# Hybrid mLSTM and S5 step: four edits, the last normalisation step of the heads moved to VectorE among them

## The chip, the cores and the metric

The program runs on one core of a Trainium2 chip. The metric is the device time of one execution in microseconds; the median of three runs of the kernel before stands for it. The engines are TensorE (PE), VectorE (DVE), ScalarE (ACT), GpSimd (POOL) and SyncE (SP). PEld is TensorE's loading of weights, which overlaps its matmuls. SP computes nothing: it issues all transfers (DMAs) of this program.

## What is computed

A decoder layer over 1024 prompt tokens and 8 × 4 sample tokens, in float32, with an mLSTM half (4 heads of 128) and an S5 half (32 groups of 16 channels):

```python
a = rmsnorm(h, ln_mix)                      # h * rsqrt(mean(h*h) + 1e-6) * ln_mix
x_m, z_m, o_m, i_pre, f_pre, x_s, z_s = split(a @ w_in)
x_conv, conv_new = causal_conv(x_m, state_conv, conv_w, conv_b)   # conv_new: the last 3 rows of x_m
x_conv = silu(x_conv)
hA, C1, n1, m1 = mlstm_chunkwise(q, k, v, i_t, logf, C0, n0, m0)  # h = num / max(|qn|, exp(-m))
hA = hA * sigmoid(o_m)
hA = (hA - mean(hA)) * rsqrt(var(hA) + EPS) * ln_head             # per head
hA = (hA + skip_a * x_conv) * silu(z_m)
yB, sre1, sim1 = s5_scan(x_s, ...)
yB = gelu(yB); yB = yB * sigmoid(yB @ w_glu + b_glu) * silu(z_s)
h = h + concat(hA, yB) @ w_out
h = h + sigmoid(h @ w_ple_gate) * rmsnorm(p @ w_ple, ln_ple)
```

The final rmsnorm of h and the new states are the outputs.

## The kernel before

Products with weights are made of three matmuls: a weight and its operand are each split into a rounded high part and the rest (`mm3`, L122 to L125: high·high, low·high, high·low). ACT writes the high part, POOL or DVE subtracts it from the raw tile for the low one (L115, L116, and `wload`, L1342 and L1345).

The stages follow one another:

- **Start.** Nine row tiles of x are loaded, normalised and transposed (`x_tile`, L150 to L180). The first tile comes in two halves (ACT squares L164, DVE and POOL make the factor `rr` L166 to L168, DVE multiplies by `rr` and by `ln_row` L170); later tiles go in one piece (ACT L157, then `rsqrt`, a DVE step L55 and a POOL power L56, then DVE L159). PE transposes into `tpx` (L176), ACT and DVE split into `aTh` and `aTl` (L178, L179), and the projection o (`ps_o`) begins. `ln_row` holds ln_mix on all 128 partitions: one DMA of 512 KB reads the same row 128 times (L297), between the loads of the first x tile and of the first weights `raw_o`.
- **S5, units u = 0 to 7.** Per unit DVE builds tables, PE transposes them (`s5_in`, tile `tpW`, L561), scans run on DVE, DVE writes the state tile `xs_` (L645, L646), PE multiplies it out into `py` (L655, L656). Between these PE has other work from a list of fillers (projection matmuls), in measured helpings: FILL_A, FILL_B and FILL_C columns (`take`). After some units a step of the generator `gate` runs (`if u in (0, 1, 4, 6): next(gate)`), which turns the gate values into tables. Its step after u = 4 copies the sample tokens' gates into `gs` (L798, L799), transposes them with PE into `tps` (L803), copies them out with DVE into `sr` (L804), and transposes three more tiles into `tpk` (L807). `tps` lies in the PSUM pool psT (one buffer) that `tpW` uses as well; `tpk` lies in psG (one buffer).
- **mLSTM heads,** the pair (0, 1) and then (2, 3) (`turns`), with the sample heads between them. After its chunks a head is normalised by `lnorm`: reciprocal of the denominator, DVE's statistics (L1209, L1211), small vectors (L1212 to L1216, with `rsqrt` on DVE and POOL inside), and last a pass over the 128x128 tiles, out = in · scale + bias with a scale and a bias per partition, on ACT (L1218), eight chunks per head in two halves of four. PE transposes the result (`tph`, L1180), DVE adds the skip part (`sk`, L1183). The conv state of the prompt, three columns per head, is copied by DVE out of `xm` into `pcn` (L1102); `xm` is itself loaded from the DRAM tile `d_xm`.
- **GLU.** Matmuls into `ps_g`, ACT's tanh `tg` (L1040), DVE (L1042), POOL's product `zg` (L1044), and at the end of a column block ACT's `mXh` (L1055) and DVE's `mXl` (L1056).
- **Output.** w_out, then w_ple and w_ple_gate over eight row tiles, with their weights loaded and split ahead.

The order of instructions on every engine is fixed when the program is built, by a scheduler that plays the program through with estimated times; on PE the S5 and mLSTM stages are in the order of the code instead. All DMAs go through the one queue of SP in that fixed order, so a transfer that waits for its data holds up those behind it.

Of the kernel before, what the change touches and what calls it, by code (L numbers as in the profile page):

```python
# [8 lines left out]
F32 = mybir.dt.float32  # L9
# [20 lines left out]
def tile_hymba(ctx: ExitStack, tc: tile.TileContext, d: dict, o: list):  # L30
# [4 lines left out]
    def dma(out, in_):  # L35
        nc.sync.dma_start(out, in_)  # L36
# [107 lines left out]
    def x_load(i):  # L144
        xt = xp.tile([128, 1024], F32, tag="xt", name="xt", bufs=5)
        for q in range(1 if i else 2):
            w = 1024 if i else 512
            dma(xt[:128 if i < 8 else 32, w * q:w * q + w], x_src(i)[:, w * q:w * q + w])
        return xt
# [143 lines left out]

    xts = []
    ow = []
    xts.append(x_load(0))
    dma(ln_row, bcast(d["ln_mix"], 1024))  # L297
    ow.append(o_w(0, 0))
    xts.append(x_load(1))
    ow.append(o_w(0, 1))  # L300
# [2 lines left out]
    dma(bgr[:, 0:4], bcast(d["b_igate"], 4))  # L303
    dma(bgr[:, 4:8], bcast(d["b_fgate"], 4))
    xts.append(x_load(3))
    for i in range(9):
        if i + 4 < 9:
            xts.append(x_load(i + 4))
        x_tile(i, xts[i])
        o_tile(0, ow, i)  # L310
        if i in (1, 4, 8):
            s5_x(0, LOC[i][0])
# [420 lines left out]
    def gates_g():  # L733
# [64 lines left out]
        V.tensor_copy(gs[:, 0], gates[:32, 0:4, 8])  # L798
        V.tensor_copy(gs[:, 1], lf[:32, :, 8])  # L799
        sr = gt_([4, 2, 32], "sr")  # L800
        tp = pt([4, 2, 32], "tps")
        for i in range(2):
            T.transpose(tp[:, i, :], gs[:, i, :], ident[:32, :32])  # L803
        V.tensor_copy(sr, tp)  # L804
        tp = pg([128, 3, 32], "tpk")
        for i, t_ in enumerate((g_, wl_, en_)):
            T.transpose(tp[:, i, :], t_, ident[:32, :32])  # L807
# [117 lines left out]
    with tc.manual_schedule(engines={mybir.EngineType.PE}):  # L925
        gate = gates_g()
        ins = [s5_in(u) for u in range(8)]
        outs = [s5_out(u) for u in range(8)]
        parts = {}
        runs = []  # L930

        def start(u, WV):
            runs.append(s5_run(u, WV, lambda: parts[u]))
            prod(runs[u])

        prod(ins[0])
        WV = prod(ins[0])
        prod(outs[0])  # L940
        tabs = prod(outs[0])
        with tc.high_priority():
            parts[0] = (*tabs, *s5_rot(0))
        start(0, WV)
        prod(ins[1])
        prod(outs[1])
        for u in range(8):
            prod(runs[u])
            if u < 7:
                WV = prod(ins[u + 1])  # L950
            take(FILL_A)
            if u < 7:
                start(u + 1, WV)
                tabs = prod(outs[u + 1])
                with tc.high_priority():
                    parts[u + 1] = (*tabs, *s5_rot(u + 1))
            if u < 6:
                prod(ins[u + 2])
            take(FILL_B)
            prod(runs[u])  # L960
            prod(runs[u])
            if u < 6:
                prod(outs[u + 2])
            take(FILL_C)
            if u in (0, 1, 4, 6):
                next(gate)
        end = s5_final()
        for n in (5000, 3000, 3000, 0):
            prod(end)
            if n:  # L970
                take(n)
# [102 lines left out]
    def mtile_xm(h):  # L1074
        xm = pxm.tile([128, 1027], F32, tag="xm", name="xm", bufs=2)
        V.memset(xm[:, 0:3], 0.0)
        dma(xm[:, 3:], d_xm[h])

        xc = (mlx if h < 2 else mly).tile([128, 1024], F32, tag="xc", name="xc", bufs=2)
        A.activation(xc, xm[:, 0:1024], AF.Identity, bias=cvb[:, h:h + 1], scale=cvw[:, h:h + 1])  # L1080
        for j in range(1, 4):
            V.scalar_tensor_tensor(xc, xm[:, j:j + 1024], cvw[:, 4 * j + h:4 * j + h + 1], xc, op0=MUL, op1=ADD)
        for q in range(2):
            tt_ = mlx.tile([128, 512], F32, tag="ctmp", name="ctmp", bufs=1)
            A.activation(tt_, xc[:, 512 * q:512 * q + 512], AF.Tanh)
            V.scalar_tensor_tensor(xc[:, 512 * q:512 * q + 512], tt_, 1.0, xc[:, 512 * q:512 * q + 512],
                                   op0=ADD, op1=MUL)
        yield
        v1 = ml.tile([128, 8, 129], F32, tag="v1", name="v1", bufs=2)
        V.memset(v1[:, :, 128:129], 1.0)  # L1090
        xmc[h] = (v1, xc)
        for t in range(2):
            ps = pv([128, 4, 128], "vps")
            for c in range(4):
                cc = 4 * t + c
                T.matmul(ps[:, c, :], xm[:, 3 + 128 * cc:131 + 128 * cc], wv[:, h, :], start=True, stop=True)
            A.copy(v1[:, 4 * t:4 * t + 4, 0:128], ps)
            yield

        V.tensor_copy(xsm[:, h, :, 0:3], scT[:, h, :].rearrange("p (b j) -> p b j", j=3))  # L1100
        V.tensor_copy(pcn[:, h, 0:24].rearrange("p (b j) -> p b j", j=3), xsm[:, h, :, 4:7])
        V.tensor_copy(pcn[:, h, 24:27], xm[:, 1024:1027])  # L1102
        a_ = ml.tile([128, 2, 8, 4], F32, tag="csm", name="csm", bufs=1)
        A.activation(a_[:, 0], xsm[:, h, :, 0:4], AF.Identity, bias=cvb[:, h:h + 1], scale=cvw[:, h:h + 1])
        for j in range(1, 4):
            V.scalar_tensor_tensor(a_[:, 0], xsm[:, h, :, j:j + 4], cvw[:, 4 * j + h:4 * j + h + 1], a_[:, 0],
                                   op0=MUL, op1=ADD)
        A.activation(a_[:, 1], a_[:, 0], AF.Tanh)
        V.scalar_tensor_tensor(xcs[:, h, :].rearrange("p (b t) -> p b t", t=4), a_[:, 1], 1.0, a_[:, 0],
                               op0=ADD, op1=MUL)  # L1110
        yield
# [88 lines left out]
    def lnorm(hs, qn, enm, p, n):  # L1200

        w_ = [ml.tile([128, n], F32, tag=f"ln{i}", name=f"ln{i}", bufs=2) for i in range(5)]
        V.scalar_tensor_tensor(w_[0], qn, -1.0, qn, op0=MUL, op1=MAX)
        V.tensor_tensor(w_[0], w_[0], enm, op=MAX)
        V.reciprocal(w_[0], w_[0])
        st_ = ml.tile([128, n, 6], F32, tag="bst", name="bst", bufs=2)
        mv = ml.tile([128, n, 2], F32, tag="bmv", name="bmv", bufs=2)
        for c in range(n):
            V.bn_stats(st_[:, c, :], hs[:, c, :])  # L1209
        for c in range(n):  # L1210
            V.bn_aggr(mv[:, c, :], st_[:, c, :])  # L1211
        V.scalar_tensor_tensor(w_[1], w_[0], 0.25, w_[0], op0=MUL, op1=MUL)  # L1212
        V.tensor_tensor(w_[1], w_[1], mv[:, :, 1], op=MUL)
        rsqrt(w_[2], w_[1], 1.0, EPS, w_[3])
        V.scalar_tensor_tensor(w_[2], w_[0], 0.5, w_[2], op0=MUL, op1=MUL)
        V.scalar_tensor_tensor(w_[4], mv[:, :, 0], -1.0, w_[2], op0=MUL, op1=MUL)  # L1216
        for c in range(n):
            A.activation(hs[:, c, :], hs[:, c, :], AF.Identity, bias=w_[4][:, c:c + 1], scale=w_[2][:, c:c + 1])  # L1218

    xmc = {}  # L1220

# [445 lines left out]
```

## Time and profile before

| | us |
|---|---|
| runs | 668.5, 662.63, 663.2 (median 663.2) |
| profiled execution, its own time | 665.62 |
| its span in the trace | 663.7 |
| PE busy | 611.8 (92%) |
| DVE busy | 441.0 (66%) |
| ACT busy | 266.1 (40%) |
| POOL busy | 147.6 (22%) |

The span begins with the first and ends with the last instruction of the trace; 1.9 us of the execution lie outside it. The mean granted clock of PE was 0.981. In the rows below a timeline row is one instruction, or several of a kind that follow each other (x4), with its start and its duration; in brackets stands how long its engine had been idle before it and what ended the wait. PEclk is the granted clock of PE as a share of full speed.

### The profile page before, as it was taken

The page shows a single profiled execution, that of the slowest core. Times are in us where ns is not written, and L with a number is a line of the kernel's source. Part 1 is how long each engine was busy: PE and PEld are TensorE (multiplying, and loading weights), DVE is VectorE, ACT ScalarE, POOL GpSimd, SP SyncE. Part 2 cuts the span into 40 slices and gives each one's busy share as a digit, 9 for nine tenths or more (in the row PEclk, how much of TensorE's full clock was granted, in tenths as well). Part 3 has the DMA queues.
Part 4 walks back from the last instruction along what each step waited for, and adds up shares of the span by engine and source line. Part 5 has one row for each costly group of instructions (what it writes and reads, how often), then busy time and mean ns, then how long its engine had stood idle before and what let it go on. Part 6 is the DMA issues. An engine that isn't in the chain of part 4 may idle for free. (4 is left out here: it accounts for less than half of the span.)

```text
span 663.7 us, 11597 instructions
## 1 busy us (share of the span) xinstructions
PE 611.8 (92%) x4068; PEld 538.3 (81%) x4068; DVE 441.0 (66%) x1297; ACT 266.1 (40%) x655; POOL 147.6 (22%) x165
## 2 busy tenths in 40 slices
PE   3999999999989998887989996899999999999995
PEld 2999998999979996776978796767888876788885
DVE  4877878999999944985657588834222335576444
ACT  5553743333434455444341536533112225443332
POOL 6730200000000003024323536842001113110000
PEclk9999999999989997998999997999999999999998
DMA  8811453455543439363634654766241273412111
GB/s 286 238 57 33 113 162 90 131 145 153 146 118 97 111 80 267 92 195 108 172 112 123 186 171 145 256 209 214 74 143 71 89 250 126 150 49 103 64 64 63
DMA packets 111983, 90.53 MB, mean 136 GB/s; under 512 B 33519, under 2 KB 94339, under 8 KB 111926
## 3 DMA queue, kind: packets, MB, share of 16 engines
q1 hardware_dynamic: 111926, 89.80, 45.2%
q8 instruction: 32, 0.52, 0.3%
q14 instruction: 25, 0.20, 0.1%
HBM read 62.19 MB, written 27.58 MB: 135 GB/s over the span
## 5 line engine op out<-in xcount | busy, mean ns | idle before, releaser
L1595 PE MATMUL po<-wgh,hTh 128*128 128x512 f32 (+1 forms) x136 | 52.3, 385 | 0.1
L1489 DVE TENSOR_TENSOR xt<-xt,po 128x512 f32<-128x512 f32 x16 | 11.0, 687 | 61.5 <-PE po L1488 58.1
L1596 PE MATMUL po<-wgl,hTh 128*128 128x512 f32 (+1 forms) x136 | 51.1, 378 | 0.0
L1597 PE MATMUL po<-wgh,hTl 128*128 128x512 f32 (+1 forms) x136 | 51.1, 379 | 0.0
L123 PE MATMUL ps_o<-hi_o,aTh 128*128 128x264 f32 (+2 forms) x136 | 41.0, 302 | 0.7 <-ACT aTh L178 0.7
L124 PE MATMUL ps_o<-lo_o,aTh 128*128 128x264 f32 (+2 forms) x136 | 39.8, 293 | 1.4 <-POOL lo_o L116 1.4
L125 PE MATMUL ps_o<-hi_o,aTl 128*128 128x264 f32 (+2 forms) x136 | 40.0, 294 | 0.2 <-DVE aTl L179 0.2
L123 PE MATMUL ps_zs<-aTh,hi_zs 128*128 128x256 f32 (+2 forms) x96 | 39.5, 411 | 0.0
L123 PE MATMUL ps_xm<-aTh,hi_xm 128*128 128x256 f32 (+2 forms) x96 | 34.8, 363 | 0.0
L123 PE MATMUL ps_zm<-aTh,hi_zm 128*128 128x256 f32 (+2 forms) x96 | 32.7, 341 | 0.0
L1488 PE MATMUL po<-woh,mlo 128*128 128x512 f32 x80 | 32.7, 409 | 0.0
L123 PE MATMUL ps_xs<-aTh,hi_xs 128*128 128x256 f32 (+2 forms) x96 | 31.4, 327 | 1.0 <-ACT xs L287 1.0
L1487 PE MATMUL po<-wol,mh 128*128 128x512 f32 x80 | 31.9, 398 | 0.0
L125 PE MATMUL ps_zm<-aTh,lo_zm 128*128 128x256 f32 (+2 forms) x96 | 31.7, 330 | 0.0
L124 PE MATMUL ps_zm<-aTl,hi_zm 128*128 128x256 f32 (+2 forms) x96 | 31.7, 330 | 0.0
L125 PE MATMUL ps_xm<-aTh,lo_xm 128*128 128x256 f32 (+2 forms) x96 | 31.5, 328 | 0.0
L1486 PE MATMUL po<-woh,mh 128*128 128x512 f32 x80 | 31.5, 394 | 0.0
L125 PE MATMUL ps_zs<-aTh,lo_zs 128*128 128x256 f32 (+2 forms) x96 | 31.4, 327 | 0.0
L124 PE MATMUL ps_zs<-aTl,hi_zs 128*128 128x256 f32 (+2 forms) x96 | 31.4, 327 | 0.0
L124 PE MATMUL ps_xm<-aTl,hi_xm 128*128 128x256 f32 (+2 forms) x96 | 31.4, 327 | 0.0
L124 PE MATMUL ps_xs<-aTl,hi_xs 128*128 128x256 f32 (+2 forms) x96 | 31.4, 327 | 0.0
L125 PE MATMUL ps_xs<-aTh,lo_xs 128*128 128x256 f32 (+2 forms) x96 | 31.1, 324 | 0.0
(591 smaller groups left out, 1923.5 us busy)
## 6 DMA issues: line engine op xcount, KB each, us to landing
xt<-in_x_prompt SPq DMA_DIRECT2D x15, 512.0 KB
Wraw<-in_w_out SPq DMA_DIRECT2D x16, 256.0 KB
Wraw<-in_w_ple_gate SPq DMA_DIRECT2D x16, 256.0 KB
d_h<-xt SPq DMA_DIRECT2D x8, 512.0 KB
h_t<-d_h SPq DMA_DIRECT2D x8, 512.0 KB
out<-g_t SPq DMA_DIRECT2D x14, 256.0 KB
mt<-d_m SPq DMA_DIRECT2D x10, 256.0 KB
d_us<-xs SPq DMA_DIRECT2D x32, 72.0 KB
```

What stands on the lines that cost most here:

```text
L123: T.matmul(ps, wh, xh, start=first, stop=False)
L124: T.matmul(ps, wh, xl, start=False, stop=False)
L125: last_mm[0] = T.matmul(ps, wl, xh, start=False, stop=last).ins
L1486: T.matmul(ps, mh[:, k % 4, :], hi, start=k == 4, stop=False)
L1487: T.matmul(ps, mh[:, k % 4, :], lo, start=False, stop=False)
L1488: T.matmul(ps, mlo[:, k % 4, :], hi, start=False, stop=k == 3)
L1489: V.tensor_tensor(xt[:, cs], xt[:, cs], ps, op=ADD)
L1595: T.matmul(ps[:, :b - a], hTh[i][:, k, :], hi[:, ws], start=k == 4, stop=False)
L1596: T.matmul(ps[:, :b - a], hTh[i][:, k, :], lo[:, ws], start=False, stop=False)
L1597: T.matmul(ps[:, :b - a], hTl[i][:, k, :], hi[:, ws], start=False, stop=k == 3)
```

## The change

There are four edits. (1) ln_mix is loaded once, 4 KB on one partition, and spread over 128 partitions by two matmuls with a column of ones; DVE copies the two halves from PSUM into `ln_row`. (2) The transposes of the sample gates are a step of `gate` of their own, one S5 unit earlier, and their PSUM tile comes from psG instead of psT. (3) The three conv state columns of each head come into `pcn` by a DMA from `d_xm` instead of a DVE copy out of `xm`. (4) The last step of `lnorm` is a `tensor_scalar` on DVE instead of an `activation` on ACT.

```diff
-    dma(ln_row, bcast(d["ln_mix"], 1024))
+    one_p = xp.tile([1, 128], F32, tag="xn", name="one_p", bufs=4)
+    V.memset(one_p, 1.0)
+    ln1 = xp.tile([1, 1024], F32, tag="xn", name="ln1", bufs=4)
+    dma(ln1, bcast(d["ln_mix"], 1024, 1))
...
     xts.append(x_load(3))
+    for q in range(2):
+        ps = pv([128, 512], "tpl")
+        T.matmul(ps, one_p, ln1[:, 512 * q:512 * q + 512], start=True, stop=True)
+        V.tensor_copy(ln_row[:, 512 * q:512 * q + 512], ps)
...
-        tp = pt([4, 2, 32], "tps")
+        tp = pg([4, 2, 32], "tps")
         for i in range(2):
             T.transpose(tp[:, i, :], gs[:, i, :], ident[:32, :32])
         V.tensor_copy(sr, tp)
+        yield
         tp = pg([128, 3, 32], "tpk")
...
-            if u in (0, 1, 4, 6):
+            if u in (0, 1, 3, 4, 6):
                 next(gate)
...
-        V.tensor_copy(pcn[:, h, 24:27], xm[:, 1024:1027])
+        dma(pcn[:, h, 24:27], d_xm[h, :, 1021:1024])
...
         for c in range(n):
-            A.activation(hs[:, c, :], hs[:, c, :], AF.Identity, bias=w_[4][:, c:c + 1], scale=w_[2][:, c:c + 1])
+            V.tensor_scalar(hs[:, c, :], hs[:, c, :], w_[2][:, c:c + 1], w_[4][:, c:c + 1], op0=MUL, op1=ADD)
```

Since the scheduler orders the engines anew, more moves than the edited lines. In the rows of the order, line numbers of the kernel after are 7 (up to L1102) or 8 higher than those of the kernel before.

On PE, after S5 unit 4, the kernel before has the sample transposes ahead of `tpk` and of the next unit's `tpW`:

```order
L125 MATMUL ps_zm_2622<-aTh_106,lo_zm_2518 128x416
L803 MATMUL tps<-ident,gs 4x32 x2
L807 MATMUL tpk<-ident,g__2031 128x32
L807 MATMUL tpk<-ident,wl__2056 128x32
L807 MATMUL tpk<-ident,en__2057 128x32
L561 MATMUL tpW<-ident,wt 128x128 x4
L123 MATMUL ps_zm_2780<-aTh_104,hi_zm_2776 128x256
L124 MATMUL ps_zm_2780<-aTl_107,hi_zm_2776 128x256
```

In the kernel after, the first piece is the end of unit 3 and the second the end of unit 4:

```order
L125 MATMUL ps_xm<-aTh_106,lo_xm_2320 128x416
L810 MATMUL tps<-ident,gs 4x32 x2
L568 MATMUL tpW<-ident,wt 128x128 x4
L123 MATMUL ps_zm_2538<-aTh_104,hi_zm_2534 128x256
L124 MATMUL ps_zm_2538<-aTl_107,hi_zm_2534 128x256
```

```order
L125 MATMUL ps_zm_2639<-aTh_106,lo_zm_2535 128x416
L815 MATMUL tpk<-ident,g__2040 128x32
L815 MATMUL tpk<-ident,wl__2065 128x32
L815 MATMUL tpk<-ident,en__2066 128x32
L568 MATMUL tpW<-ident,wt 128x128 x4
L123 MATMUL ps_zm_2789<-aTh_104,hi_zm_2785 128x256
```

The two transposes into `tps` have moved one unit up, ahead of an earlier `tpW`, and `tpk` has stayed.

On DVE, ahead of unit 5's second half of `xs_` (the row L646 before, L653 after), the kernel before has:

```order
L640 TENSOR_TENSOR v_2755<-zi,rti 128x256
L641 TENSOR_TENSOR v_2756<-zr,rti 128x256
L642 TENSOR_TENSOR v_2757<-zi,rtr 128x256
L822 TENSOR_TENSOR sg<-sr,sb 4x32
L551 TENSOR_TENSOR u_2928<-pdr,Cs 128x576
L552 TENSOR_TENSOR u_2929<-pdi,Cj 128x576
L645 TENSOR_TENSOR xs__2751<-v_2754,v_2755 64x2x128 x2
L716 SCALAR_TENSOR_TENSOR ztmp<-ztmp,zc 128x256
L599 TENSOR_TENSOR rti<-rBr,rAi 128x256
L599 TENSOR_TENSOR rtr<-rBr,rAr 128x256
L646 TENSOR_TENSOR xs__2751<-v_2756,v_2757 64x2x128 x2
```

and the kernel after:

```order
L647 TENSOR_TENSOR v_2764<-zi,rti 128x256
L648 TENSOR_TENSOR v_2765<-zr,rti 128x256
L649 TENSOR_TENSOR v_2766<-zi,rtr 128x256
L836 COPY smo<-sm__2722 4x8
L586 SCALAR_TENSOR_TENSOR ks<-dsel,Dt,ks 128x16
L558 TENSOR_TENSOR u_2937<-pdr,Cs 128x576
L559 TENSOR_TENSOR u_2938<-pdi,Cj 128x576
L1396 TENSOR_TENSOR smb<-smb,smask 32x128
L652 TENSOR_TENSOR xs__2760<-v_2763,v_2764 64x2x128 x2
L606 TENSOR_TENSOR rti<-rBr,rAi 128x256
L606 TENSOR_TENSOR rtr<-rBr,rAr 128x256
L653 TENSOR_TENSOR xs__2760<-v_2765,v_2766 64x2x128 x2
```

A copy of the sample gates' result (`smo`), `ks` and the sample mask (`smb`, which is loaded from DRAM) now stand ahead of unit 5's `xs_`; the sample gates' scan `sM` has gone further ahead, to the unit before.

On ACT, at the end of the second pair of heads, the kernel before has the two halves of L1218 among the tanh of the GLU and the weight casts `woh`:

```order
L1040 ACTIVATE tg<-ps_g,hcols 128x288
L1306 COPY sob<-tpn 32x128
L1218 ACTIVATE qd<-qd,ln_5205,ln_5203 128x128 x4
L1342 CAST woh_5756<-Wraw 128x512
L1218 ACTIVATE qd<-qd,ln_5244,ln_5242 128x128 x4
L1473 CAST mh<-mt 128x512
L1055 ACTIVATE mXh_5352<-zg 128x1024
L1040 ACTIVATE tg<-ps_g,hcols 128x288
```

and the kernel after:

```order
L1048 ACTIVATE tg<-ps_g,hcols 128x288
L1314 COPY sob<-tpn 32x128
L1350 CAST woh_5765<-Wraw 128x512
L1481 CAST mh<-mt 128x512
L1063 ACTIVATE mXh_5361<-zg 128x1024
L1048 ACTIVATE tg<-ps_g,hcols 128x288
```

The two groups of four are gone, and `mh`, `mXh` and the next tanh follow directly on the casts. `mXh` still reads POOL's `zg`.

## Rows read from the trace of the kernel before

**Rows 1.** The page: busy time, share of the span and instructions of each engine.
```profile
PE 611.8 (92%) x4068; PEld 538.3 (81%) x4068; DVE 441.0 (66%) x1297; ACT 266.1 (40%) x655; POOL 147.6 (22%) x165
```

**Rows 2.** Windows: stretch in us, length, busy time (instructions) by engine, PEclk, DMA share, GB/s.
```profile
100.00:235.00 135.00, 131.86 (x1074) 125.38 (x1073) 130.87 (x344) 51.09 (x142) 0.63 (x6) 0.99 0.48 123
400.00:450.00 50.00, 38.76 (x324) 32.41 (x324) 36.22 (x62) 25.44 (x52) 33.97 (x29) 0.93 0.61 194
450.00:650.00 200.00, 199.68 (x1012) 158.95 (x1010) 84.23 (x152) 62.06 (x149) 28.24 (x31) 1.00 0.34 115
```

**Rows 3.** Timeline of PE, first 20 us: start us, us, instruction [idle before <-releaser].
```profile
13.69 0.59 PE L124 MATMUL ps_o<-lo_o,aTh 128*128 128x264 f32 x1 [1.44 <-POOL lo_o L116]
...
17.87 1.94 PE L176 MATMUL tpx<-ident,xn 128*128 128x128 f32 x8 [1.17 <-DVE rr L55]
```

**Rows 4.** Timeline of ACT, POOL and DVE in the same stretch.
```profile
10.06 1.07 ACT L115 CAST hi_o<-raw_o 128x1056 fp32r<-128x1056 f32 x1 [4.42 <-DMA raw_o<-in_w_in]
...
11.21 2.43 POOL L116 TENSOR_TENSOR lo_o<-raw_o,hi_o 128x1056 fp32r<-128x1056 f32 x1 [4.74 <-ACT hi_o L115]
...
14.19 2.45 POOL L116 TENSOR_TENSOR lo_o<-raw_o,hi_o 128x1056 fp32r<-128x1056 f32 x1
...
8.22 1.42 DVE L170 SCALAR_TENSOR_TENSOR xn<-xt,rr,ln_row 128x512 f32<-128x512 f32 x2 [2.39 <-DMA ln_row<-in_ln_mix]
...
14.18 3.54 DVE L159 SCALAR_TENSOR_TENSOR xn<-xt,rr,ln_row 128x1024 f32<-128x1024 f32 x1 [0.84 <-POOL rr L56]
```

**Rows 5.** S5 units 4 and 5: timeline of PE and DVE, one window.
```profile
187.84 0.66 PE L561 MATMUL tpW<-ident,wt 128*128 128x128 f32 x4 [2.92 <-DVE sr L804]
...
201.40 0.39 PE L655 MATMUL py<-us,tz 128*128 128x136 f32 x2
...
197.60 0.87 DVE L646 TENSOR_TENSOR xs__2751<-v,v 64x256 f32<-64x256 f32 x2
...
188.00:192.00 4.00, 4.00 (x23) 4.00 (x23) 4.00 (x9) 0.59 (x1) 0.00 (x0) 0.57 0.06 23
```

**Rows 6.** First pair of heads: timeline of PE.
```profile
290.51 0.36 PE L1292 MATMUL sups<-svm,skw 96*128 96x258 f32 x1 [1.60 <-DVE sc L1294]
...
302.91 1.48 PE L1180 MATMUL tph<-ident,qd 128*128 128x128 f32 x4 [3.35 <-ACT qd L1218]
...
305.32 1.09 PE L1180 MATMUL tph<-ident,qd 128*128 128x128 f32 x4
```

**Rows 7.** The same stretch: timeline of DVE and ACT, one window.
```profile
284.29 0.17 DVE L1102 COPY pcn<-xm 128x3 f32<-128x3 f32 x1 [1.47 <-DMA xm<-d_xm]
...
302.36 3.19 ACT L1218 ACTIVATE qd<-qd,ln,ln 128x128 f32<-128x128 f32 x8 [2.67 <-DVE ln L1216]
...
305.00:308.00 3.00, 2.96 (x11) 2.13 (x11) 1.10 (x3) 0.55 (x2) 3.00 (x3) 0.53 0.05 18
```

**Rows 8.** Second pair of heads, end: timeline of PE, ACT, POOL and SP.
```profile
407.90 0.61 PE L123 MATMUL ps_g<-yh,hi_g 128*128 128x288 f32 x1 [5.93 <-ACT tg L1040]
...
404.35 1.65 ACT L1218 ACTIVATE qd<-qd,ln,ln 128x128 f32<-128x128 f32 x4 [1.11 <-DVE ln L1216]
...
406.41 1.05 ACT L1055 ACTIVATE mXh<-zg 128x1024 fp32r<-128x1024 f32 x1
407.37 0.48 ACT L1040 ACTIVATE tg<-ps_g,hcols 128x288 f32<-128x288 f32 x1
...
402.55 1.65 POOL L1044 TENSOR_TENSOR zg<-tg,zg 128x256 f32<-128x256 f32 x2
...
436.32 0.39 SPq L36 DMA_DIRECT2D d_m<-zg  x1
```

**Rows 9.** Groups of instructions: count | busy us, mean ns; the last one with min/median/max ns.
```profile
L1218 ACT ACTIVATE qd<-qd,ln,ln 128x128 f32<-128x128 f32 x32 | 13.0, 484 | 4.9 <-DVE ln L1216 4.8
...
L1172 DVE SCALAR_TENSOR_TENSOR qd<-so,nu 128x128 f32<-128x128 f32 x32 | 8.8, 275 | 0.0
...
L1129 PE MATMUL qps<-xc,Gm x16: 590/592/1222, 255.2 to 364.6; 128*128 128x512 f32 x16
```

## Prediction

> **What bounds the kernel now.** I read the page first. PE is busy 611.8 of 663.7 us, so all its idle time together is 51.9 us, and no edit touches a large share of PE's work [rows 1]. What the change can win are PE's stops and the stretches at half clock behind them. The windows by stage come next. In the S5 stage PE and DVE are both nearly full (131.86 and 130.87 of 135 us); between 400 and 450 PE works 38.76 of 50; from 450 to 650 it works 199.68 of 200, so what is won or lost by 450 reaches the end one to one [rows 2]. The timeline of PE then gives the stops by place, and that of the engine named as releaser what it did before: the start [rows 3, 4], one S5 unit [rows 5], the first pair of heads [rows 6, 7], the end of the second pair [rows 8]. In all four places a line of the diff stands in or near the chain.
>
> **Edit 1, ln_mix.** It removes a 512 KB broadcast, for which DVE waited until 8.22 [rows 4]. It adds a 4 KB load, a memset, two fp32 matmuls of 128x512 and two DVE copies. The nearest row for the matmuls is L1129, 128x512 in two records of 0.59 us at full and up to 1.22 at half clock [rows 9]: 2.4 us each if the clock is still low, 4.9 for both, begun when the first weights are not there yet. The copies have DVE's half of a 1.42 us pair as the nearest row, 0.7 each [rows 4]. PE's first product that needs the low weights waits for POOL's `lo_o` (11.21 to 13.64), this for ACT's cast at 10.06, and this for the load of `raw_o` [rows 3, 4]. `raw_o`, as large as `ln_row` and behind it in the queue, landed 1.84 us after it [rows 4]; without those 512 KB I let it land 1.9 earlier. Next late are the two spread matmuls and copies: x's second half can be multiplied at about 10.2, transposed at 10.9 and cast at 12, a little ahead of what `lo_o` then needs. So the start gains at most 1.9, and loses 1 if the spread is slower than that. I take 1.3. The DVE work has cover, as DVE is idle in this stretch while it waits.
>
> **Edit 2, the sample transposes.** In S5 unit 4 PE stands 2.92 us at `tpW`, because `tps` held the one buffer of psT until DVE's late copy `sr`; then it runs at 0.57 of its clock for 4 us, mostly the lower level of 1.2 GHz, which costs 1.7 more [rows 5]. Both go with the edit: 4.6 us on PE, the upper end. But DVE is full in this stage. It ended unit 5's `xs_` at 198.47 and PE came to read it at 201.40 [rows 5], a slack of 2.9. If PE comes 4.6 earlier, at 196.8, `xs_` is what is late, and the changed order puts `smo`, `ks` and `smb` ahead of it, some 0.15 to 0.2 us each by rows of that size, and `smb` may wait for its load. So `xs_` ends near 199.3 and PE waits 2.5: 2.1 are left. If the clock falls again behind that wait, as it fell behind 2.92, another 1.7 goes, and 0.4 is left. I take 1.2, with 0 and 4.6 as ends.
>
> **Edit 3, the conv columns.** Four DVE copies of 0.17 go, one of which held DVE 1.47 us for the load of `xm`, in front of the products `sc` that PE's `sups` waits for [rows 6, 7]. Four DMAs of 1.5 KB come onto SP's queue, each some 0.4 us of issue like its neighbour [rows 8]; they read DRAM that the load of `xm` before them reads too, so they add no wait of their own, and `pcn` is used only at the end. Its gain is counted with the next edit, since both meet in the first pair of heads.
>
> **Edit 4, L1218.** ACT loses 32 instructions with 13.0 us and one more of the sample; eight in a row took 3.19, so each holds ACT 0.39 [rows 9, 7]. DVE gets 33 `tensor_scalar` of 128x128, which this trace does not have in float32 from SBUF at that size. From above, the nearest row is L1172, same size with two tensor inputs, 0.275 us [rows 9]; beside a running POOL instruction it can be more: L159 took 3.54 beside `lo_o`, where two halves of the same work took 1.42 without it [rows 4]; 0.275 stretched by that 2.5 is 0.7. From below I let it be half of 0.275, as if the second input cost half the time. I take 0.2, between them, 6.6 us in all, and 0.7 beside POOL. Off the stops it is hidden by DVE's idle time.
>
> The Trainium skill speaks against this edit here: the GPSIMD Engine Reference, under Specifications, says that POOL's way to SBUF is shared with VectorE and that the two contend where a DVE instruction runs in a two-port mode or has two SBUF inputs. By VectorE: DVE Perf Modes (The perf-mode tier table) a float32 `tensor_scalar` from SBUF is a two-port one, an ACT pass is not. The stretched L159 [rows 4] agrees for two inputs; no row shows it for a `tensor_scalar`. By that rule the eight at the end of the second pair cost up to 0.7 instead of 0.2 each, 4 us more on DVE there; the case where that decides is the third rival.
>
> What it does to PE in the first pair: PE's stop of 3.35 at 302.91 ends with the first of ACT's eight at 302.36; the second `tph` begins at 305.32, and 305 to 308 runs at 0.53 [rows 6, 7]. In the new order the first head's vectors and its four `tensor_scalar` stand some 1.5 us further up on DVE (an estimate: the sample's copies and products of 0.2 to 0.4 each that were ahead now follow), the second head's behind the first's `sk`. I put the first `tph` at 301.2 and the second at 304.6. That is 0.7 at the second, and 1.0 of the 1.4 that half clock costs. Further up, with the stall at 284.29 gone and `sc` ahead of two long conv steps, I take 1.3 of the 1.60 stop at 290.51, and 0.5 at the step after it. Together 3.5, with 0 and 6 as ends.
>
> At the end of the second pair PE waits 5.93 us for a tanh at 407.37. Ahead of it on ACT stand two groups of L1218 (the second 404.35 to 406.0) and `mXh`, which needs POOL's `zg` (402.55 to 404.20) [rows 8]. Without L1218 `mXh` runs at 404.2 and the tanh 0.96 behind it as before; PE started 0.53 behind the tanh, so at 405.7 instead of 407.9. The gain is 2.2, with 0 and 4 as ends; the stop stays over 3 us and the half clock behind it too. Two other places with L1218 give 0.5 together. On the other side DVE gets about 1.8 us of new work in these last 15 us, and the new orders bring small waits that I cannot see: 1.2 off.
>
> **Sum.** 1.3 + 1.2 + 3.5 + 2.2 + 0.5 − 1.2 = 7.5. The profiled execution took 665.62, 663.7 of it span, which gives 658.1. The median of the runs, 663.2, is 0.4% below that execution, so against it I predict 656. With each term at its nearer end this case reaches from −4 to −11 us, 652 to 659.
>
> **Rivals.** *The next limit takes the gains.* DVE is full in S5, and at the end of the second pair `mXh` waits for POOL whatever ACT does [rows 2, 8]. If PE loses its clock again at unit 5 and `zg` does not come earlier, edit 2 gives 0.4 and edit 4 there less than 1; with 1.3 from the start and 1.5 from the first pair, minus 1.2, it is 3: 662.6, or 660. For it speaks that both engines show no slack; against it that the stops have a named line that is gone.
>
> *All the stops close.* If DVE follows everywhere and the clock stays up, it is 4.6, 6, 4 and the start's 1.9, minus 2 for DVE: 14.5, 651, or 649. Against it stands DVE's full S5 stage.
>
> *The end of the second pair gets slower.* POOL is busy 33.97 and DVE 36.22 of the 50 us from 400 [rows 2]. Eight `tensor_scalar` at 0.7 beside POOL are 5.6 us in front of DVE's part of `zg`, against the 1.6 of eight at 0.2; POOL's `zg` and then the store of it to `d_m`, issued at 436.32 [rows 8], move with them, and the last w_out loads behind that store on SP as well. With two products of POOL more in front of it, by the scheduler's new order (1.65 each), it costs 4.0 and 3.3 there, while the start and the first pair bring 1.3 and 1.5 as in the first rival: 4.5 slower, 670, or 668. It decides from where that store is issued later than in the trace before. Against it: DVE has 14 of the 50 us free.
>
> **How the numbers follow.** The forecast has a chance of 0.50, the first rival 0.25, the second 0.12, the third 0.13. About 1% (6.6 us) is what a measurement of this kernel can tell from no change. The forecast's middle, 7.5, is just over that, so some 0.31 of its 0.50 count as faster, with the second rival and a little of the first 0.47; slower by over 1% is most of the third, 0.10; the rest, 0.43, is within. The range of 648.5 to 664 takes in the first rival and the better part of the second, and leaves out the third.
>
> **What would show it.** Right: `lo_o` starts before 10; no stop at `tpW` in unit 4, but one of 2 to 3 us at `py` of unit 5; the DVE `tensor_scalar` near 0.2; the first `tph` stop under 2 us; ACT's tanh in front of the 5.93 stop waiting for `mXh`, that for POOL. Wrong: PE stops at the spread matmuls' copies, a stop at `py` as long as the one that went, `tensor_scalar` over 0.5, or the store of `zg` later than 436 us.

## The result and the profile after

| | before | after |
|---|---|---|
| median of the runs, us | 664.3 | 668.4 |
| profiled execution, its own time | 665.62 | 666.65 |
| its span | 663.7 | 664.9 |

The ratio of after to before is 1.0058, with a 95% interval of 1.0035 to 1.0081: 0.6% slower, where 1% faster was forecast and 664.0 was the top of the range. (The median of before is over more runs than the three ahead of the prediction.) The profiled execution of after is the fastest of its runs (they reach 672.33), so its trace shows less loss than the median has.

The page of after, where [rows 1] had it before:

```profile
PE 614.1 (92%) x4072; PEld 536.8 (81%) x4072; DVE 450.2 (68%) x1329; ACT 253.9 (38%) x622; POOL 147.2 (22%) x165
```

ACT has lost 12.2 us, DVE has gained 9.2, and PE has four records more, those of the spread. Two windows of the first pair of heads (length, busy time by engine in the order of [rows 2], PEclk, DMA share, GB/s):

```profile
296.00:300.00 4.00, 0.65 (x4) 0.30 (x3) 3.89 (x11) 0.00 (x0) 2.58 (x3) 0.93 0.08 29
300.00:304.00 4.00, 3.21 (x11) 2.49 (x12) 2.34 (x6) 0.72 (x1) 2.54 (x3) 0.50 0.39 131
```

From 296 to 300 PE works 0.65 us of 4 while DVE works 3.89 and ACT nothing at all: the engine that lost the work stands idle while the one that got it is full. At 300 PE comes back at half clock.

Held against each other matmul by matmul, the two traces of PE show where the time went. After stands ahead of before by 3.3 us at the start of S5 (97.41 against 100.67), by 6.3 at its end, by 2.2 when the heads begin, by 7.9 at the first `tph`, by 4.5 at the second, by 1.6 at 392, by 1.7 at 442, and behind by 0.85 at 461 and 1.2 at the end of the span. So the change is over 6 us ahead at the end of S5 and some 8 at the first `tph`. It loses some 4 us ahead of the heads, near 5 from the first `tph` to 306, 3.2 between 329 and 368, and the rest behind 411, the end of the w_out loads last. Timeline rows of after at these places, PE first, then the engines it waits for:

```profile
4.20 3.75 PE L311 MATMUL tpl<-ln,one_p 1*128 1x512 f32 x4 [4.20 <-DMA ln<-in_ln_mix]
...
181.86 0.66 PE L568 MATMUL tpW<-ident,wt 128*128 128x128 f32 x4
...
195.26 0.47 PE L663 MATMUL py<-xs__2760,cs 128*128 128x136 f32 x2 [0.95 <-DVE xs__2760 L653]
...
252.95 1.13 PE L1137 MATMUL qps<-xc,Gm 128*128 128x512 f32 x2 [2.95 <-ACT v L1105]
...
289.55 0.38 PE L1238 MATMUL sqk<-xcs,wq 128*128 128x32 f32 x2 [1.83 <-DVE sc L1302]
...
294.98 1.10 PE L1188 MATMUL tph<-ident,qd 128*128 128x128 f32 x4 [0.24 <-DVE qd L1226]
...
300.79 1.15 PE L1188 MATMUL tph<-ident,qd 128*128 128x128 f32 x4 [4.14 <-DVE qd L1226]
...
403.31 0.40 PE L123 MATMUL ps_g<-yh,hi_g 128*128 128x288 f32 x1 [2.71 <-ACT tg L1048]
408.00 0.39 PE L124 MATMUL ps_g<-yl,hi_g 128*128 128x256 f32 x1 [2.46 <-DVE yl L1034]
...
445.64 0.43 PE L1361 MATMUL po<-Wraw,mt 128*32 128x128 f32 x8 [1.25 <-DMA Wraw<-in_w_out]
...
9.43 2.42 POOL L116 TENSOR_TENSOR lo_o<-raw_o,hi_o 128x1056 fp32r<-128x1056 f32 x1 [3.49 <-ACT hi_o L115]
...
194.69 0.87 DVE L653 TENSOR_TENSOR xs__2760<-v,v 64x256 f32<-64x256 f32 x2
...
296.38 1.31 DVE L1251 COPY sxv<-xsm 128x32 f32<-128x32 f32 x3
...
298.47 0.75 DVE L1191 SCALAR_TENSOR_TENSOR sk<-tph,hcols,sk 128x512 f32<-128x512 f32 x1
299.14 0.15 DVE L1224 SCALAR_TENSOR_TENSOR ln<-bmv,ln 128x4 f32<-128x4 f32 x1
299.33 2.09 DVE L1226 TENSOR_SCALAR qd<-qd,ln,ln 128x128 f32<-128x128 f32 x4
...
400.94 3.21 DVE L1226 TENSOR_SCALAR qd<-qd,ln,ln 128x128 f32<-128x128 f32 x4
...
404.60 1.11 DVE L1226 TENSOR_SCALAR qd<-qd,ln,ln 128x128 f32<-128x128 f32 x4
...
296.22 1.27 POOL L1163 TENSOR_TENSOR qd<-qp,dcb 128x512 f32<-128x512 f32 x1 [1.52 <-issue]
...
299.30 1.26 POOL L1194 TENSOR_TENSOR sk<-sk,zt 128x512 f32<-128x512 f32 x1
...
400.93 1.65 POOL L1052 TENSOR_TENSOR zg<-tg,zg 128x256 f32<-128x256 f32 x2
```

The stops of [rows 5] and [rows 6] at `tpW` and at the first `tph` are gone. In their place PE stands 2.95 us at 252.95 for `v` (1.90 in the trace of before), 4.14 us ahead of the second `tph`, and in two halves, 2.71 and 2.46 us, where [rows 8] had one of 5.93. The rows of DVE show a second thing: the four passes of L1226 take 1.11 us at 404.60, but 2.09 at 299.33 and 3.21 at 400.94, and both times a product on POOL begins within 0.03 us of them. The group says it in one line (min, median, max in ns):

```profile
L1226 DVE TENSOR_SCALAR qd<-qd,ln,ln x32: 332/342/1319, 294.6 to 405.4; 128x128 f32<-128x128 f32 x32
```

### The profile page after: what moved, and what is told of

Read it like the earlier page. It is cut to its first block, busy times and chain, and to the rows that moved or that the text cites. A ratio compares the mean times of both kernels' runs of the same rounds, so it can differ in the third digit from the quotient of the medians.

```text
span 664.9 us, 11614 instructions
## 1 busy us (share of the span) xinstructions
PE 614.1 (92%) x4072; PEld 536.8 (81%) x4072; DVE 450.2 (68%) x1329; ACT 253.9 (38%) x622; POOL 147.2 (22%) x165
## 4 chain that ended last, share of the span: by engine, by line
PE 59%; DVE 12%; issue 12%; DMA 9%; ACT 2%; SPq 2%; POOL 2%; POOLq 0%; DVEq 0%; ACTq 0%
PE po L1603 4%; PE po L1496 4%; PE po L1494 4%; PE po L1495 4%; PE po L1604 4%; PE po L1605 4%; PE ps_o L123 2%; DMA nmb<-d_row 2%; PE ps_o L124 2%; PE ps_o L125 2%; PE ps_xs L123 2%; PE ps_xs L124 2%; SPq L36 2%; PE ps_xs L125 2%; PE ps_zs L123 2%
```

## The experiments

Unless a run says otherwise, nothing of the computation is left out; only the engine, the order or the form of an instruction differs. All ratios are to the kernel before on the same chip. The kernels were spread over four chips, and the difference of two ratios has an uncertainty of some 0.4%.

### One edit at a time

The edits are those of the diff ahead, each applied alone to the kernel before.

Edit 1 (ln_mix):

> The kernel before with edit 1 alone (ln_mix spread by a product). Theory A (gains are given back at fixed points, the last of them the DRAM round trip of zg and the w_out loads at 436 to 450): PE reaches the first S5 tpW about 3.3 us earlier, as in the kernel after (97.4 against 100.7), but the dense output stage starts within 1 us of the kernel before, time within 1.5 us of it. Theory B (each place counts one to one, edit 4 alone makes it slower): 2.5 to 3.5 us faster. Theory C (any edit makes a new order of instructions, which costs or wins a few us by itself): up to 4 us either way, with a place that has nothing to do with ln_mix.

Measured: 0.9949 (0.9916 to 0.9982).

Edit 2 (sample transposes):

> The kernel before with edit 2 alone (sample transposes one unit up, in another PSUM pool). Theory A: no stop at tpW of unit 4 and no half clock behind it, 3 us ahead at the end of S5, time within 1.5 us of the kernel before. Theory B: 3 us faster. Theory C: up to 4 us either way.

Measured: 0.9926 (0.9900 to 0.9952).

Edit 3 (conv columns):

> The kernel before with edit 3 alone (conv state columns by a load). Theories A and B: within 1 us of the kernel before. Theory C: up to 4 us either way, from an order that changed elsewhere.

Measured: 1.0004 (0.9980 to 1.0027).

Edit 4 (last step of the normalisation):

> The kernel before with edit 4 alone (last step of the heads' normalisation on VectorE). Theory A: the stop before the tanh at 402 to 408 shrinks by about 2 to 3 us, the time stays within 1.5 us. Theory B: 3 to 5 us slower, from DVE in the two pairs of heads. Theory C: up to 4 us either way.

Measured: 1.0088 (1.0054 to 1.0121).

So two edits are worth 0.5 and 0.7%, the third nothing, and the fourth, from which the forecast had the largest share of its gain, costs 0.9%.

### Edits 1 to 3 together, and after again

> Edits 1, 2 and 3 without edit 4. Theory A (edit 4 puts eight instructions of 0.26 us on DVE in front of the xw copy that PE's sps waits for, and loses there what edits 1 and 2 win): 0.9% to 1.3% faster than the kernel before, the stop of PE ahead of sps at 368 back to 0.6 us. Theory B (the gains of edits 1 and 2 do not add up, since both meet the same later limit, the DRAM round trip of zg and the w_out loads): 0.3% to 0.8% faster.

Measured: 0.9871 (0.9841 to 0.9901), 657.9 us against 666.5, and the lowest ratio of all that ran. Edits 1 and 2 add up: it is the version to keep. And the kernel after, timed against the same runs of before:

> The kernel after once more, on the same chip as the other three: 0.3% to 0.8% slower than the kernel before. A stop of about 1.8 us ahead of sps in the second pair of heads, and, where the clock falls behind it or behind the stops at 403 to 410, a time 2 to 5 us above the first profile of it.

Measured: 1.0044 (1.0008 to 1.0081). Edit 4 on top of the others therefore costs 1.75%, some 12 us. Timeline rows of edits 1 to 3, first pair of heads, to be held against those of after:

```profile
298.15 0.68 PE L1188 MATMUL tph<-ident,qd 128*128 128x128 f32 x4
...
299.76 1.17 PE L1188 MATMUL tph<-ident,qd 128*128 128x128 f32 x4 [0.37 <-DVE sk L1191]
...
298.24 0.35 DVE L1251 COPY sxv<-xsm 128x32 f32<-128x32 f32 x3
298.49 0.16 DVE L1223 SCALAR_TENSOR_TENSOR ln<-ln,ln 128x4 f32<-128x4 f32 x1
298.69 0.16 DVE L1224 SCALAR_TENSOR_TENSOR ln<-bmv,ln 128x4 f32<-128x4 f32 x1
298.87 0.75 DVE L1191 SCALAR_TENSOR_TENSOR sk<-tph,hcols,sk 128x512 f32<-128x512 f32 x1
...
298.90 1.64 ACT L1226 ACTIVATE qd<-qd,ln,ln 128x128 f32<-128x128 f32 x4
```

With the pass on ACT the stop ahead of the first `tph` is gone as well, and the second waits 0.37 us. The 3.35 us of [rows 6], which edit 4 was to shorten, needed no edit 4: the scheduler's new order has the two heads' vectors one after the other instead of side by side, and ACT's passes run beside DVE. The traces of edits 1, 2 and 3 alone have no stop over 0.4 us at either `tph` too, so any of the new orders closed it, and the ratio of a single edit is not the price of its own mechanism alone.

### Where edit 4 costs it

Edit 4 in a part of the heads, by a flag of `lnorm`:

```diff
+            if vec:
+                V.tensor_scalar(hs[:, c, :], hs[:, c, :], w_[2][:, c:c + 1], w_[4][:, c:c + 1], op0=MUL, op1=ADD)
+            else:
                 A.activation(hs[:, c, :], hs[:, c, :], AF.Identity, bias=w_[4][:, c:c + 1], scale=w_[2][:, c:c + 1])
```

Second pair, first half (`vec=h > 1 and t == 0`), alone on the kernel before:

> The kernel before with edit 4 only in the first halves of heads 2 and 3, the eight instructions beside xw. Theory A: half or more of the loss of edit 4 alone, 3 to 5 us slower than the kernel before, with PE's stop ahead of sps at 370 grown from 0.6 to about 1.8 us and half clock behind it. If the loss of edit 4 is spread over all 33 instructions: 1 to 2 us slower.

Measured: 1.0013 (0.9986 to 1.0040). The mechanism is there: PE waits 1.82 us for `xw`, behind the passes, where other kernels show 0.6:

```profile
372.83 1.16 PE L1142 MATMUL sps<-qp,xc 128*128 128x128 f32 x8 [1.82 <-DVE xw L1137]
```

But 1.2 us is all, so this is not where most of the loss is.

Second pair, second half (`vec=h > 1 and t == 1`), with edits 1 to 3:

> Edits 1, 2 and 3, and edit 4 only in the second halves of heads 2 and 3, eight instructions that stand on ACT in front of the tanh at 402 to 408. Theory A: as fast as edits 1 to 3 or up to 2 us faster, since no xw stands behind these eight and PE's stop of 5.9 shrinks to under 3. Theory B: no better than edits 1 to 3. If DVE work itself is what costs: slower than edits 1 to 3 by 1 to 2 us.

Measured: 0.9922 (0.9898 to 0.9946), 0.5% behind edits 1 to 3. The tanh stop of 5.42 us there falls to 2.25, and two others come up behind it:

```profile
399.58 0.40 PE L123 MATMUL ps_g<-yh,hi_g 128*128 128x288 f32 x1 [2.25 <-ACT tg L1048]
404.62 0.58 PE L124 MATMUL ps_g<-yl,hi_g 128*128 128x256 f32 x1 [2.27 <-DVE yl L1034]
...
442.09 2.54 PE L1364 MATMUL po<-Wraw,mt 128*32 128x128 f32 x32 [2.33 <-DMA Wraw<-in_w_out]
```

First pair, first half (`vec=h < 2 and t == 0`), with edits 1 to 3:

> Edits 1, 2 and 3, and edit 4 only in the first halves of heads 0 and 1. Theory A2 (on DVE the second head's four stand behind the first head's skip product and beside POOL's work, so that PE's second tph comes late and the clock falls behind that stop): PE's stop ahead of the second tph near 300 is 3 to 4.5 us instead of 0.4, 2 to 4 us slower than edits 1 to 3, which is 0.7% to 1.0% faster than the kernel before. If edit 4 costs by its number of instructions alone: under 1 us slower than edits 1 to 3.

Measured: 0.9996 (0.9975 to 1.0016). Against edits 1 to 3 these eight passes alone cost 1.25%, nearly all that those win. (Edits 1 to 3 ran on another chip. On the chip of this kernel they ran with the queue changed alone, see below, with a ratio of 0.9932; against that the cost is 0.65%.) The stop ahead of the second `tph` is 4.14 us as in after, and the next 8 us run at a clock of 0.57 and 0.58.

### More priority for the pass

The last three steps of `lnorm` under the scheduler's high priority, in the kernel after:

> All four edits, with the last three steps of the heads' normalisation given priority in the scheduler's order. Theory A2: where these steps move ahead of the skip product on DVE, PE's stop ahead of the second tph shrinks from 4.1 to under 2.5 and the kernel is 2 to 4 us faster than the kernel after; where xw falls further behind, the stop ahead of sps at 368 grows by up to 1 us. If the loss comes from DVE time and not from the order: same as the kernel after within 1 us.

Measured: 1.0038 (1.0008 to 1.0068), as after. The second head's vector still stands behind `sk`, and the stop is 4.14 us again: priority did not move the rows, so this says nothing on what another order would bring. Edit 4 alone on the kernel before has such an order; there both passes stand on DVE ahead of the first `sk`:

```profile
301.40 1.10 PE L1180 MATMUL tph<-ident,qd 128*128 128x128 f32 x4 [2.06 <-DVE qd L1218]
...
305.12 1.11 PE L1180 MATMUL tph<-ident,qd 128*128 128x128 f32 x4 [2.06 <-DVE sk L1183]
...
302.22 2.06 DVE L1218 TENSOR_SCALAR qd<-qd,ln,ln 128x128 f32<-128x128 f32 x4
304.32 0.75 DVE L1183 SCALAR_TENSOR_TENSOR sk<-tph,hcols,sk 128x512 f32<-128x512 f32 x1
```

PE then waits 2.06 us twice, 4.12 together where before waits 3.35, and reaches the second `tph` 0.2 us earlier than before. So this order splits the wait and does not take it away. What edit 4 alone loses, its trace loses further on: 4.3 us between 333 and 374, and more behind 410.

### Which head carries it

One head of the first pair each, with edits 1 to 3:

> Edits 1 to 3, and edit 4 for the first head of the first pair alone; the second head's pass stays on ACT. Theory S (the loss in the first pair is the second head's pass, which on DVE stands behind the first head's sk): the first head's four tensor_scalar are ready for PE without a wait, so this is within 1.5 us of edits 1 to 3 (ratio to before 0.986 to 0.991) and PE's stop ahead of the second tph stays under 1.2 us. Theory B (any pass taken from ACT to DVE costs its 1.1 us in the full DVE queue and a share of half clock): half of the 6 to 8 us, ratio 0.993 to 0.997.

Measured: 0.9980 (0.9959 to 1.0002).

> Edits 1 to 3, and edit 4 for the second head of the first pair alone. Theory S: most of the loss of both heads together, 3 to 7 us against edits 1 to 3, ratio 0.992 to 0.999, a stop of 2.5 us or more ahead of the second tph. Theory B: half of it, as for the first head alone, 0.993 to 0.997 with a stop of 1 to 2 us. If the ratio is below 0.991, neither holds and both heads are needed for the long stop.

Measured: 0.9915 (0.9884 to 0.9945). Theory S fell, and so did the even split of B: the first head's pass alone costs 1.1%, the second's 0.4%, the latter not clear of noise. In the second's trace the second head's vectors stand ahead of the first `sk` (298.61 and 298.82), and PE stands 1.03 us ahead of the second `tph` and 0.83 inside it. The trace of the first shows why it costs more; the second head's pass is on ACT here:

```profile
303.54 1.63 PE L1188 MATMUL tph<-ident,qd 128*128 128x128 f32 x4 [3.22 <-ACT qd L1229]
...
298.26 1.10 DVE L1227 TENSOR_SCALAR qd<-qd,ln,ln 128x128 f32<-128x128 f32 x4
...
300.06 1.31 DVE L1254 COPY sxv<-xsm 128x32 f32<-128x32 f32 x3
...
302.81 0.15 DVE L1224 SCALAR_TENSOR_TENSOR ln<-bmv,ln 128x4 f32<-128x4 f32 x1
...
303.00 1.65 ACT L1229 ACTIVATE qd<-qd,ln,ln 128x128 f32<-128x128 f32 x4 [4.47 <-DVE ln L1224]
```

The windows behind it:

```profile
300.00:304.00 4.00, 0.78 (x4) 0.25 (x2) 2.88 (x9) 1.00 (x3) 2.79 (x3) 0.95 0.04 14
304.00:308.00 4.00, 4.00 (x14) 2.98 (x14) 0.93 (x2) 1.37 (x3) 2.74 (x3) 0.50 0.40 131
308.00:312.00 4.00, 4.00 (x34) 3.53 (x32) 2.00 (x9) 0.72 (x1) 0.00 (x0) 0.70 0.42 131
```

ACT stands 4.47 us idle for one vector from DVE, the second head's bias (L1224). Counted from the last product `nmb` of the first head on DVE, that vector begins 5.14 us later here (297.67 to 302.81) and 1.81 with edits 1 to 3 (296.88 to 298.69). The 3.33 us between are: 1.03 for the four passes, 0.97 more for the three copies (1.22 instead of 0.25 to the next row), and 1.35 for `skw`, `sv` and `sk`, which the new order has ahead of the vector. With the 3.2 us stop come 3.2 us of half clock (4 us of PE work at 0.50 and 4 at 0.70). Together that is about what this kernel loses there: against edits 1 to 3 it is 0.5 us late at the first `tph` and 6.65 at 310.5.

### What the passes wait for on DVE

The bias as a second tensor input, everything else on DVE in the same order:

```diff
-                V.tensor_scalar(hs[:, c, :], hs[:, c, :], w_[2][:, c:c + 1], w_[4][:, c:c + 1], op0=MUL, op1=ADD)
+                V.scalar_tensor_tensor(hs[:, c, :], hs[:, c, :], w_[2][:, c:c + 1], w_[4][:, c:c + 1].to_broadcast([p, 128]), op0=MUL, op1=ADD)
```

> Edits 1 to 3, and edit 4 for the first pair's prompt heads with a scalar_tensor_tensor (the bias as a second tensor input, broadcast along the row) in place of the tensor_scalar; DVE's order is the same, row by row, as in the kernel with tensor_scalar there, whose stop ahead of the second tph was 4.14 us. Theory P (a DVE instruction with one tensor input waits for a POOL instruction that is under way: the copy took 1.14 instead of 0.17, the first tensor_scalar 1.32 instead of 0.34; one with two tensor inputs doesn't): no instruction of the pass over 0.5 us, the stop 0.8 to 1.1 us shorter, 3.0 to 3.4, and 1 to 2.5 us less in all, ratio 0.995 to 0.999. Theory Q (order alone, POOL plays no part): the stop stays within 0.3 us of 4.1 or grows, since nothing has moved, and the ratio is within 0.2% of 0.9996.

Measured: 0.9986 (0.9961 to 1.0012).

```profile
304.14 1.17 PE L1188 MATMUL tph<-ident,qd 128*128 128x128 f32 x4 [4.21 <-DVE qd L1227]
...
302.61 2.17 DVE L1227 SCALAR_TENSOR_TENSOR qd<-qd,ln,ln 128x128 f32<-128x128 f32 x4
...
302.59 1.26 POOL L1194 TENSOR_TENSOR sk<-sk,zt 128x512 f32<-128x512 f32 x1
```

The form changes nothing: with two tensor inputs the pass takes 2.17 us beside POOL. Theory P fell in its second half, that such a form doesn't wait; the wait itself is still there. The same form in all 33 places of after:

> The kernel after with the same scalar_tensor_tensor in all 33 places. Theory P: the second tph's stop at 3.0 to 3.4 instead of 4.14, and 1 to 4 us less than the kernel after: ratio 0.999 to 1.003. Theory Q: as the kernel after, 1.003 to 1.008, or slower, if the two-input form is the longer one.

Measured: 1.0001 (0.9973 to 1.0030). The stop ahead of the second `tph` is 4.21 us, so what is won against after is won elsewhere; its interval still touches that of after taken again, and what wins it stays open.

The three copies on ACT, which is idle there; DVE's other rows keep their order:

```diff
-            V.tensor_copy(xv[:, 1, i].rearrange("p (b t) -> p b t", t=4), xsm[:, h, :, 3:7])
+            A.copy(xv[:, 1, i].rearrange("p (b t) -> p b t", t=4), xsm[:, h, :, 3:7])
```

> Edits 1 to 3, edit 4 for the first pair's prompt heads, and the three sample copies (sxv from xsm) on ACT, which is idle there, instead of DVE; the rest of DVE's order is the same row by row. In the kernel without this the copies took 1.31 us ahead of the second head's vectors, one of them 1.14 beside POOL's product qd. Theory C (it is the length of DVE's chain, the copies' 1.31 us in it): the second head's vectors come 1.3 us earlier and the stop ahead of the second tph falls from 4.14 to 2.7 to 3.0, the time by 1.3 to 2.5 us, ratio 0.996 to 0.998. Theory D (what takes the 1 us is POOL's product under way, whichever DVE instruction from SBUF comes to it first): the wait goes over to the next such instruction, the vector ln of 128x4, which then shows about 1 us instead of 0.15; the stop falls by the copies' own 0.35 at most, to 3.7 to 4.1, and the ratio is 0.998 to 1.0005.

Measured: 0.9987 (0.9956 to 1.0017).

```profile
302.58 1.15 PE L1188 MATMUL tph<-ident,qd 128*128 128x128 f32 x4 [3.88 <-DVE qd L1227]
...
298.43 1.13 DVE L1223 SCALAR_TENSOR_TENSOR ln<-ln,ln 128x4 f32<-128x4 f32 x1
...
298.27 1.27 POOL L1163 TENSOR_TENSOR qd<-qp,dcb 128x512 f32<-128x512 f32 x1 [1.56 <-ACT sxv L1254]
```

Theory D holds. The vector L1223 has 4 columns and took 0.16 us with edits 1 to 3; here it shows 1.13, and ends with POOL's product. The stop falls by 0.26 us alone. The next DVE instruction from SBUF pays, whatever its size.

> The kernel after with the same three copies per head on ACT. Theory C: 1.3 to 2.5 us less than the kernel after, ratio 1.001 to 1.003. Theory D: within 0.5 us of it, 1.004 to 1.006.

Measured: 1.0027 (0.9995 to 1.0059), in theory C's range, with an interval that holds D's as well. Its trace speaks for D: the vector shows 1.13 again and the stop is 3.89 us. So the time alone doesn't tell the two apart here, the rows do.

### The queue at the last w_out loads

The rival of the prediction saw the last loads behind the store of `zg` on SP. Two kernels issue the loads of `mt` that wait for this store from ACT:

```diff
-            dma(mt, src[:, :, off:off + 128].rearrange("k p t -> p k t"))
+            (nc.scalar if x else nc.sync).dma_start(mt, src[:, :, off:off + 128].rearrange("k p t -> p k t"))
```

Edits 1 to 3 with it:

> Edits 1, 2 and 3, with the two loads behind the store of zg (mt from d_m1) issued by ACT instead of SP, so that the last four w_out loads do not queue behind them. If the stop at 441 to 445 is set by that queue: the four loads are issued 3 us earlier, PE's stop of 1.1 goes, 1 to 2 us faster than edits 1 to 3. If the loads' own buffers or ACT's casts set it: no change.

Measured: 0.9932 (0.9906 to 0.9957).

> The kernel after with the same two loads issued by ACT. If the last stop with its half clock takes 2 to 3 us in the kernel after because the w_out loads queue behind the landing of the store: 2 to 4 us faster than the kernel after, about the time of the kernel before. Otherwise the same as the kernel after.

Measured: 1.0024 (0.9994 to 1.0054). No gain in either. With edits 1 to 3 the stop at the last loads does go, but one of the same kind opens 15 us earlier, and the span of the two profiled executions is the same to 0.1 us (658.6 and 658.7). By the ratios it is 0.6% behind edits 1 to 3, which ran on another chip; whether the queue or the chip makes this difference is not shown.

```profile
426.34 0.43 PE L1361 MATMUL po<-Wraw,mt 128*32 128x128 f32 x8 [2.36 <-DMA Wraw<-in_w_out]
```

## Why the prediction was wrong

**Start.** There is a gain, as put, but I put it too small, and it does not come by the chain that I gave. `lo_o` starts at 9.43, 1.8 us earlier, as put; the four spread matmuls take 3.75 us, not 4.9, and the first `tpx` follows at 7.88. But PE's first product with `lo_o` starts at 13.59, only 0.1 us before that of the kernel before (13.69), because x's second half has become late. I had it multiplied at 10.2 and transposed at 10.9. Its product on DVE starts at 10.76, behind a step of the next tile that waits for ACT, and takes 1.63 us beside `lo_o` on POOL, where the first half took 0.75:

```profile
12.45 1.12 PE L176 MATMUL tpx<-ident,xn 128*128 128x128 f32 x4 [3.45 <-DVE xn L170]
...
10.76 1.63 DVE L170 SCALAR_TENSOR_TENSOR xn<-xt,rr,ln_row 128x512 f32<-128x512 f32 x1
```

The lead opens behind it: the stop of 1.17 us at 17.87 [rows 3] is 0.23 us, and the single rows of `ps_o` take 0.29 us from 17.52 on, where before they take 0.42 until 20.71. Why they are shorter sooner is not shown. At the first S5 tables after is 3.3 us ahead, and the kernel with edits 1 to 3 1.8 (98.88 against 100.67), where 1.3 stood in the sum. That a gain came at all is in part luck.

**S5.** Right that the `tpW` stop goes and that `py` of unit 5 waits for `xs_` instead; its size was off: 0.95 us, not 2.5. After was 3.26 us ahead at 97 us and 6.28 at 199, so this term is 3.0, not 1.2. I had let `xs_` come 0.8 us later for the rows put ahead of it. Set against the start of the stage it is 0.35 later (194.69 against 197.60, of which 3.26 is the start), and the clock did not fall behind the short wait.

**Edit 3.** No time of its own, as put: 1.0004. The stop of 1.60 us for `sc` at 290.51, from which I took 1.3, is gone, but PE waits 1.83 for the same tile one step on, at 289.55 (1.13 there before), so some 0.9 of the two stays.

**What is late next ahead of the heads.** Not in the sum at all. The lead falls from 6.3 to 2.2 us between 199 and 252.95. In this stretch after has three stops: 0.81 us for `zc` at 218.38, and 1.55 and 2.95 us for `v` at 244.93 and 252.95. Before has the last of them alone, and shorter:

```profile
255.18 1.13 PE L1129 MATMUL qps<-xc,Gm 128*128 128x512 f32 x2 [1.90 <-ACT v L1097]
```

Together that is 3.4 of the 4.1 us. The other kernels show 1.3 to 3.4 us in the last place, and after taken again 1.89, so its length belongs to no single edit. Behind its 1.90 us before runs at 0.57 of the clock from 256 to 264; behind its 2.95 after stays at 1.00, and the lead is back at 4.9 us at 258. So the claim that what is won early reaches the end one to one was wrong already here: it held for the stage from 450, not for the stretch between.

**Edit 4, first pair: the step that failed.** I wrote: "I put the first `tph` at 301.2 and the second at 304.6", and took 0.7 and 1.0 us for it. Three things were wrong in it. The gain was not edit 4's: with edits 1 to 3 and ACT's pass both stops are already gone. I saw that the second head's rows would stand behind the first's `sk`, and priced that as a small rest of the old stop; but with ACT out, the second pass can't run beside DVE's `sk`, copies and vectors, and the first one moves all of these back. And I kept 0.2 us for a `tensor_scalar`, and 0.7 beside POOL as an upper price for the end of the second pair only, though POOL's products of the first pair (`qd` and `sk`, [rows 7] has POOL busy 3.00 of 3 us) lie in the same stretch. What it measured on top of edits 1 to 3: passes of 0.34 us, four in 1.11, two waits of 1 us for POOL, a stop of 4.14 and half clock behind it; in the kernel with these eight passes alone 1.25% (0.65% by the kernel on the same chip).

I also wrote that no row shows the wait for POOL for a `tensor_scalar`. The trace of before has such a row, 1.01 us for 128x4 where others of this line show 0.16, and it ends with POOL's product:

```profile
323.37 1.01 DVE L55 TENSOR_SCALAR ln<-ln 128x4 f32<-128x4 f32 x1
...
323.04 1.31 POOL L1125 TENSOR_TENSOR nmb<-nmb,cmask 128x512 f32<-128x512 f32 x1 [3.32 <-DMA nmb<-d_row]
```

So the price beside POOL could have been read ahead, and with it that a small instruction pays it in full.

**Edit 4, end of the second pair.** The term was right and did not stay. Without L1218 the tanh comes earlier, the stop of 5.93 falls to 2.71 (I had put 2.2 us of gain), and then PE waits 2.46 us more for `yl` on DVE, where four passes beside POOL took 3.21 and the other four 1.11. This is the mechanism of the third rival, at 0.8 per pass instead of 0.7 for the first four; its sign, a store of `zg` later than 436, did not come (434.48), and its price was not what decided the time.

The Trainium skill was right where I used it for a rival alone. The GPSIMD Engine Reference (Specifications) says that POOL's way to SBUF is shared with VectorE and contended by a DVE instruction in a two-port mode or with two SBUF inputs. The traces agree for the `tensor_scalar` (2.09 for four), the copy (1.31 for three), the two-input form (2.17) and a vector of 4 columns (1.13): all read SBUF alone. `sk`, which also reads the PSUM tile `tph`, does not wait: in the trace of before it took 0.75 us at 306.45, with POOL's product under way until 306.97. The Trainium skill's page SBUF — State Buffer (SBUF: two separate sides) adds that whoever comes second is blocked for the whole instruction of the other, and the 1.13 beside a product of 1.27 agrees. Beside POOL's power (L56) the rows differ, and they decide: in the trace of before a `tensor_scalar` of 128x4 took 0.16 us at 300.21, inside a power of 1.02 us that began at 299.92. I had weighed the rule at one place and left the first pair out.

**What stays open.** By the sums above, the first pair costs 1.25 of the 1.75% (or 0.65, by the kernel on the same chip) and the last half of the second pair 0.5; that the two and the 1.2 us at 372 add up to the whole was not tried in one kernel. Profiles of after taken twice differ in how much PE's work was slowed by half clock: 7.1 and 11.5 us, as the sum of PE's busy time times one minus the granted clock over windows of 4 us. Which stops of 1.5 to 3 us are followed by half clock is not the same in every execution, so a part of each ratio is not a fixed price of a stop. On top of edits 1 to 3, an order with both passes on DVE and the second head's vectors ahead of the first `sk` was not reached, since priority did not move them.

## What to carry to other kernels

Before work is moved from an idle engine to a busy one, look at what the idle engine did at the same time: ACT's pass cost ACT 1.64 us per head, but it ran beside DVE, and on DVE everything behind it moved back, the other head's vectors first. Take a stop's closing to an edit only after the other edits have been thought through without it, since a scheduler's new order may close it for nothing. And a small DVE instruction from SBUF that met a POOL product here cost the rest of that product, whatever its own size; look for such rows in the trace that you already have.

## What the runs showed of the hardware

- A DVE instruction of 128x4 from SBUF took 1.13 us beside a POOL product of 1.27 and 0.16 without; three copies of 128x32 took 1.31 beside one and 0.35 without. Taking the first victim out of the queue handed the wait to the next one.
- In float32 a `tensor_scalar` of 128x128 with a scale and a bias per partition showed 0.34 us, four in a row 1.11; the form with the bias as a broadcast tensor took 1.14 for four. The second input cost next to nothing, where I had let it cost half.
- Behind the stops of 3.2 to 4.2 us ahead of the second `tph`, PE ran near 0.5 of the clock for some us. That cost 2.8 us in after (3.21 us of work at 0.50 and 4.00 at 0.71), 3.2 with the first head's pass alone on DVE, and 1.4 in after with the copies on ACT (4.00 at 0.65).
